# A transformer block's last projection ended in two column halves, and the last sum of each row's mean square moved to ScalarE

## The chip, the cores and the metric

One Trainium2 chip, one core. The time is device microseconds of one execution of the whole program, and smaller is better. The kernel before was run three times: 418.63, 420.02 and 420.79 us, median 420.02 us. One further execution was profiled.

## The reference

The program computes one transformer block on 256 tokens of width 1024, and a final normalisation. All arrays are float32. Cut to what matters here:

```
x  = x + gt_m * (gated attention branches @ w_out)          # 1024 x 1024
h2 = rms_norm(x, g_ffn) * (1 + sc_f) + sh_f
u  = causal_conv(h2 @ w_up)                                  # 1024 -> 5632
y  = (gelu(u_gate) * u_val) @ w_down                         # 2816 -> 1024
out = rms_norm(x + gt_f * y, g_final)
rms_norm(x, g) = x / sqrt(mean(x*x over the 1024 columns) + 1e-6) * g
```

## The kernel before

The 256 tokens are two tiles of 128 rows, t = 0 and t = 1, with the tokens on the partitions wherever a row is summed. Float32 operands are split into a high and a low part (`wh`, `wl` for weights, made on ScalarE and VectorE; `xh`, `xl` for activations), and a product is three matmuls: high times high, high times low, low times high (`mm3`, lines 181 to 185).

The weights come through a stream of units. One unit of the stages `out` and `down` is two blocks of 128 rows by 512 columns, so it takes 2 x 3 matmuls per token tile. `Stream.mm` runs one unit for one token tile; with a stage's last unit the stage's `finish` is started, which takes the sums out of PSUM. `Stream.ahead` issues loads and splits of later units before each step. A PSUM accumulator is one bank of 512 columns; four banks go round among the stages from `out` on.

`down` has two stages, `down0` for the output columns 0 to 511 and `down1` for 512 to 1023, with 11 units each. `down0` runs both token tiles unit by unit. `down1` runs through `staggered` with a lag of 4: tile 1 follows tile 0 by four units, so that tile 0's end falls beside the last four units (24 matmuls) of tile 1. The stage `out` and the first stage of `up` are staggered in the same way.

`residual` (line 939) takes columns out of PSUM: multiply by the gate row (line 940, VectorE), add to the residual `xr` (line 941, VectorE), square with a sum over the columns (line 942, ScalarE, a second small instruction reads the accumulator). `down_put` calls it for 512 columns in `down0` and twice for 256 columns in `down1`; each time a VectorE instruction of one column (line 1077) adds the scaled sum to the one before. Then GpSimd raises the mean to the power -0.5 (line 1085), ScalarE scales the columns 0 to 511, which already hold x times g (line 1086), VectorE makes the columns 512 to 1023 (line 1088), and SyncE and ScalarE issue one output DMA of 512 columns each (lines 1087 and 1090).

`rstd_of` (line 126) is the same end for the two earlier normalisations: VectorE adds two partial sums where there are two (line 130), scales and adds 1e-6 (line 131 or 133), GpSimd raises to the power (line 135). `square` and `turn` call it for the first normalisation at the program's start, `out_put` for the one between `out` and `up`. There the rows are scaled (line 959), transposed on TensorE (line 968), modulated (lines 976 and 979) and split (lines 153 and 154) for the first matmuls of `up`.

Up to the stage `out` each engine's order is the order of the text. From there on a planner sets it when the program is built: each engine takes, of the instructions that the planner's own clock holds ready, the one of highest priority, which is the earliest in the text unless a `high_priority` block lifts it. At run time each engine keeps that order.

Of the kernel before, what the change touches and what calls it, by code (L numbers as in the profile page):

```python
# [9 lines left out]
F32 = mybir.dt.float32  # L10
F32R = mybir.dt.float32r
AF = mybir.ActivationFunctionType
ALU = mybir.AluOpType
# [4 lines left out]
P = 128  # L18
D = 1024
# [34 lines left out]
def block_kernel(ctx: ExitStack, tc: tile.TileContext, x, c, w_ada, b_ada, g_mix, w_in, w_br_moba,  # L54
# [27 lines left out]
    def slot(tag, shape, dtype, name):  # L82
        return const.tile(shape, dtype, tag=tag, name=name)
# [11 lines left out]
    nc.vector.memset(ones, 1.0)  # L95
    neghalf = const.tile([P, 1], F32, name="neghalf")
    nc.vector.memset(neghalf, -0.5)
    ident = const.tile([P, P], F32, name="ident")
    nc.gpsimd.affine_select(ident, ones, pattern=[[1, P]], base=0, channel_multiplier=-1,
                            compare_op=ALU.is_equal, fill=0.0)  # L100
# [22 lines left out]
    warm_up(12)  # L123


    def rstd_of(ss, name):

        ms = small.tile([P, 1], F32, tag="ms", name=f"ms_{name}")
        if ss.shape[1] == 2:
            nc.vector.tensor_add(ms, ss[:, 0:1], ss[:, 1:2])  # L130
            nc.vector.tensor_scalar(ms, ms, 1.0 / D, EPS, op0=ALU.mult, op1=ALU.add)
        else:
            nc.vector.tensor_scalar(ms, ss, 1.0 / D, EPS, op0=ALU.mult, op1=ALU.add)
        r = small.tile([P, 1], F32, tag="rstd", name=f"rstd_{name}")
        nc.gpsimd.tensor_tensor(r, ms, neghalf, op=ALU.pow)
        return r
# [65 lines left out]
    class Stream:  # L202
# [67 lines left out]
        def mm(self, t, u):  # L270
# [15 lines left out]
            self.events += 1  # L286
            tick()

        def mm_fm(self, u, w):
            st, k0, _, _ = self.units[u]  # L290
            first, last = k0 == 0, k0 + 2 == st.kts
            prods = [(kk, sx, wi) for kk in range(2) for sx, wi in ((st.xh, w[0]), (st.xh, w[1]), (st.xl, w[0]))]
            if first:
                st.ps = [None, None]

            def product(n, f):
                kk, sx, wi = prods[n]
                nc.tensor.matmul(st.ps[f // 2][:, f % 2 * S:(f % 2 + 1) * S],  # L298
                                 wi[:, kk * 512 + f * P:kk * 512 + (f + 1) * P], sx(k0 + kk),
                                 start=first and n == 0 and f % 2 == 0, stop=last and n == 5 and f % 2 == 1)  # L300

            for half in range(2):
                if first:
                    st.ps[half] = self.bank(f"ps_{st.nm}_{half}")
                if first or last:
                    for n in range(6):
                        for f in (2 * half, 2 * half + 1):
                            product(n, f)
                else:
                    for n in range(3 * half, 3 * half + 3):  # L310
                        for f in range(4):
                            product(n, f)
                self.left[u] -= 1
# [53 lines left out]
            for t in (None,) if st_.fm or st_.half else range(NT):  # L367
                stream.mm(t, u)

    def staggered(us, lag):  # L370

        us = list(us)
        for i in range(len(us) + lag):
            if i >= lag:
                stream.mm(1, us[i - lag])
            if i < len(us):
                stream.mm(0, us[i])
# [9 lines left out]
    def square(t):  # L387
        sq = slot(f"xn{t}", [P, D], F32, f"sq{t}")
        ss = small.tile([P, 1], F32, tag="ss1", name=f"ss1_{t}")
        nc.scalar.activation(sq, xs[t], AF.Square, accum_out=ss)  # L390
        return ss

    def turn(t, ss):
# [540 lines left out]

    xr, xn = [None] * NT, [None] * NT
    ss2 = [small.tile([P, 2], F32, tag="ss2", name=f"ss2_{t}") for t in range(NT)]
    h2 = []

    def residual(t, ps, sl, row, ss, e):
        nc.vector.tensor_mul(e, ps, row[:, sl])  # L940
        nc.vector.tensor_add(xr[t][:, sl], xr[t][:, sl], e)
        nc.scalar.activation(e, xr[t][:, sl], AF.Square, accum_out=ss)

    def out_put(i):
        def put(t, ps):
            with tc.high_priority(offset=0):
# [2 lines left out]
                sl = slice(i * 512, (i + 1) * 512)  # L949
                residual(t, ps, sl, gt_m, ss2[t][:, i:i + 1], xn[t][:, sl])  # L950
            if i == 0:
                return
            if not h2:
                h2.extend(slot(n, [P, KT, S], F32R, f"{n}_") for n in ("h2h", "h2l"))
            with tc.high_priority(offset=200):
                r = rstd_of(ss2[t], f"n2_{t}")
                for half in range(2):
                    sl = slice(half * 512, (half + 1) * 512)
                    nc.vector.tensor_scalar(xn[t][:, sl], xr[t][:, sl], r, None, op0=ALU.mult)
# [103 lines left out]
                for g in range(NF // 2)]  # L1063

    def down_put(i):
        def put(t, ps):
            n = len(down_parts[i])
            for a, w in down_parts[i]:
                col = pre[t][1]
                e = small.tile([P, 512], F32, tag="hf", name=f"fy{t}{a}", bufs=3)[:, :w]  # L1070
                residual(t, ps[:, a - i * 512:a - i * 512 + w], slice(a, a + w), gt_f, ss3[t][:, col:col + 1], e)
                first = col == 0
                pre[t][1] += 1
                if first:
                    pre[t][2] = small.tile([P, 3], F32, tag="msx", name=f"ms3_{t}")
                ms = pre[t][2][:, col:col + 1]
                nc.vector.tensor_scalar(ms, ss3[t][:, col:col + 1], 1.0 / D, EPS if first else pre[t][0],
                                        op0=ALU.mult, op1=ALU.add)
                pre[t][0] = ms
            if i == 0:  # L1080
                yo[t] = slot(f"xn{t}", [P, D], F32, f"yo{t}")
                nc.vector.tensor_mul(yo[t][:, 0:512], xr[t][:, 0:512], gfin[:, 0:512])
                return
            rs = small.tile([P, 1], F32, tag="rstd", name=f"rstd_n3_{t}")
            nc.gpsimd.tensor_tensor(rs, pre[t][0], neghalf, op=ALU.pow)
            nc.scalar.mul(yo[t][:, 0:512], yo[t][:, 0:512], rs)
            nc.sync.dma_start(out[t * P:(t + 1) * P, 0:512], yo[t][:, 0:512])
            nc.vector.scalar_tensor_tensor(yo[t][:, 512:], xr[t][:, 512:], rs, gfin[:, 512:], op0=ALU.mult,
                                           op1=ALU.mult)
            nc.scalar.dma_start(out[t * P:(t + 1) * P, 512:], yo[t][:, 512:])  # L1090
            yield 1
        return put

    pre = [[None, 0, None] for _ in range(NT)]
    down_parts = [[(0, 512)], [(512, 256), (768, 256)]]
    yo = [None] * NT
    down_units = [stream.add(Stage(f"down{i}", NF, columns(w_down, i * 512), stacked(ah), stacked(al), down_put(i)))
                  for i in range(2)]
# [45 lines left out]
    nc.gpsimd.dma_start(gfin, bass.AP(tensor=g_final.tensor, offset=g_final.offset, ap=[[0, P], [1, D]]))  # L1144
    ss3.extend(small.tile([P, 3], F32, tag="ss3", name=f"ss3_{t}") for t in range(NT))
    together(down_units[0])
    staggered(down_units[1], 4)
    drain()


# [27 lines left out]
```

## Time and profile before

| | us |
|---|---|
| median of three runs | 420.02 |
| the three runs | 418.63 to 420.79 |
| the profiled execution's own time | 418.87 |
| its span, first to last instruction | 417.1 |
| mean granted TensorE clock, share of full speed | 0.995 |

The profile's times are those of the profiled execution, from the start of its span. In the rows, PE is TensorE's matmuls, DVE VectorE, ACT ScalarE, POOL GpSimd, and SPq and ACTq are the engines' own DMA issue. A row of the timeline gives start, length, engine, line, operation and shapes, a count where several follow one another, and in brackets how long the engine had been idle before and what ended that.

### The profile page before, as it was taken

To read this page: it belongs to the slowest core of one execution; us is meant where nothing else is said; L and a number is where in the kernel's file an instruction comes from. 1 tells how busy PE (TensorE), PEld (TensorE's weight loads), DVE (VectorE), ACT (ScalarE), POOL (GpSimd) and SP (SyncE) were. 2 spreads that over 40 slices of the span, in tenths; PEclk is the share of its full clock that TensorE was granted. 3 is DMA by queue.
4 is the path that set the end of the run, shared out by engine and by line. 5 is a ranking of instruction groups with operands and counts; after the bars stand their busy time and mean duration, and the time that the engine had idled before them with its cause. 6 is when DMAs were issued, how large, how long until landed. Compare 5 with 4: busy or idle time off the path is not lost.

```text
span 417.1 us, 7453 instructions
## 1 busy us (share of the span) xinstructions
PE 402.3 (96%) x2956; PEld 369.1 (88%) x2956; DVE 315.8 (76%) x474; ACT 253.9 (61%) x405; POOL 25.9 (6%) x64
## 2 busy tenths in 40 slices
PE   7999999999999999999979999999999999999992
PEld 6778899999999999999857999999999998888881
DVE  3645579788578979999597899999978888546433
ACT  4544477787697897816375658666766676343412
POOL 4500000000000110000330000000000000000000
PEclk9999999999999999999999999999999999999997
DMA  8999998977556875876957686877566555564002
GB/s 272 335 327 332 341 323 272 334 253 258 198 179 229 262 281 173 281 239 224 321 167 240 211 263 215 264 243 250 166 212 182 202 170 170 176 242 133 21 0 101
DMA packets 75082, 94.49 MB, mean 227 GB/s; under 512 B 2573, under 2 KB 61072, under 8 KB 75047
## 3 DMA queue, kind: packets, MB, share of 16 engines
q1 hardware_dynamic: 74135, 91.82, 68.2%
q10 hardware_dynamic: 576, 1.57, 1.0%
q0 software_dynamic: 336, 0.62, 0.4%
q8 instruction: 23, 0.38, 0.4%
q14 instruction: 12, 0.10, 0.1%
HBM read 92.94 MB, written 1.06 MB: 225 GB/s over the span
## 4 chain that ended last, share of the span: by engine, by line
PE 88%; SPq 3%; DMA 3%; DVE 3%; issue 1%; ACT 1%; POOL 0%; POOLq 0%; ACTq 0%
PE ps_up L298 27%; PE ps_down L185 15%; PE ps_ga L329 6%; PE ps_gb L329 6%; PE pA L472 4%; PE ps_out L185 4%; PE ps_vb L329 3%; PE ps_qb L329 3%; PE ps_yb L329 3%; PE ps_kb L329 3%; PE ps_ya L329 3%; DMA ada<-in_w_ada_dram 2%; PE ps_up L185 2%; PE pV L477 2%; SPq L449 2%; PE cs L457 1%
## 5 line engine op out<-in xcount | busy, mean ns | idle before, releaser
L143 ACT CAST wh_up<-raw_up 128x1024 fp32r<-128x1024 f32 x44 | 46.1, 1049 | 26.6 <-PE ps_up L298 21.5
L298 PE MATMUL ps_up<-h2h__2633,wh_up 128*128 128x256 f32 x320 | 57.7, 282 | 0.0
L298 PE MATMUL ps_up<-h2h__2633,wl_up 128*128 128x256 f32 x320 | 57.4, 281 | 0.0
L298 PE MATMUL ps_up<-h2l__2634,wh_up 128*128 128x256 f32 x320 | 57.4, 281 | 0.0
L148 DVE TENSOR_TENSOR wl_up<-raw_up,wh_up 128x1024 fp32r<-128x1024 f32 x42 | 50.9, 1220 | 7.0 <-ACT wh_up L143 6.9
L298 PEld LDWEIGHTS ps_up<-h2h__2633,wh_up 128*128 128x128 f32 x320 | 46.4, 188 | 0.2
L298 PEld LDWEIGHTS ps_up<-h2h__2633,wl_up 128*128 128x128 f32 x320 | 46.3, 188 | 0.0
L298 PEld LDWEIGHTS ps_up<-h2l__2634,wh_up 128*128 128x128 f32 x320 | 46.3, 188 | 0.0
L148 DVE TENSOR_TENSOR wl_down<-raw_down,wh_down 128x1024 fp32r<-128x1024 f32 x22 | 26.9, 1224 | 25.5 <-ACT wh_down L143 25.5
L143 ACT CAST wh_down<-raw_down 128x1024 fp32r<-128x1024 f32 x22 | 23.1, 1052 | 32.1 <-PE ps_down L185 23.6
L1040 DVE SCALAR_TENSOR_TENSOR cv<-ps_up,wc,cv 128x255 f32<-128x255 f32 (+1 forms) x80 | 34.6, 477 | 1.4 <-ACT cv L1034 0.8
L185 PE MATMUL ps_down<-wh_down,hl_a 128*128 128x512 f32 x88 | 34.8, 395 | 0.0
L185 PE MATMUL ps_down<-wl_down,hh_a 128*128 128x512 f32 x88 | 34.8, 395 | 0.0
L185 PE MATMUL ps_down<-wh_down,hh_a 128*128 128x512 f32 x88 | 34.8, 395 | 0.0
L1034 ACT ACTIVATE cv<-ps_up,vc,wc 128x256 f32<-128x256 f32 x40 | 20.4, 561 | 5.9 <-PE ps_up L298 5.9
L553 ACT CAST whA<-raw_wA 128x1024 fp32r<-128x1024 f32 (+1 forms) x9 | 8.6, 952 | 21.3 <-DMA raw_wA<-in_w_in_dram 21.3
L185 PEld LDWEIGHTS ps_down<-wh_down,hl_a 128*128 128x128 f32 x88 | 16.5, 188 | 4.0
L185 PEld LDWEIGHTS ps_down<-wh_down,hh_a 128*128 128x128 f32 x88 | 16.6, 188 | 3.9
L185 PEld LDWEIGHTS ps_down<-wl_down,hh_a 128*128 128x128 f32 x88 | 16.5, 188 | 3.9
L556 DVE TENSOR_TENSOR wlA<-raw_wA,whA 128x1024 fp32r<-128x1024 f32 x8 | 9.8, 1226 | 8.5 <-ACT whA L553 8.4
L329 PE MATMUL ps_gb<-hh,wh_gb 128*128 128x256 f32 x64 | 13.2, 288 | 0.0
L329 PE MATMUL ps_ga<-hh,wh_ga 128*128 128x256 f32 x64 | 13.2, 288 | 0.0
(280 smaller groups left out, 968.6 us busy)
## 6 DMA issues: line engine op xcount, KB each, us to landing
raw_up<-in_w_up_dram SPq DMA_DIRECT2D x44, 512.0 KB, 5.3
raw_down<-in_w_down_dram SPq DMA_DIRECT2D x10, 1024.0 KB, 4.9
ada<-in_w_ada_dram SPq DMA_DIRECT2D x16, 512.0 KB, 8.1
raw_wA<-in_w_in_dram SPq DMA_DIRECT2D x8, 768.0 KB, 9.4
raw_ga<-in_w_in_dram SPq DMA_DIRECT2D x4, 1024.0 KB, 9.8
ada_gtm<-in_w_ada_dram SPq DMA_DIRECT2D x8, 512.0 KB, 5.4
ada_shf<-in_w_ada_dram SPq DMA_DIRECT2D x8, 512.0 KB, 5.0
raw_gb<-in_w_in_dram SPq DMA_DIRECT2D x4, 1024.0 KB
```

Of the source, the lines that this page charges most:

```text
L143: nc.scalar.copy(wh, t[:, a:a + 1024])
L148: eng.tensor_sub(wl, t[:, a:a + 1024], wh.bitcast(F32))
L185: nc.tensor.matmul(ps, sx(k)[:, sl], w[:, c0:c0 + n], start=first and i == 0, stop=last and i == 2)
L298: nc.tensor.matmul(st.ps[f // 2][:, f % 2 * S:(f % 2 + 1) * S], wi[:, kk * 512 + f * P:kk * 512 + (f + 1) * P], sx(k0 + kk), start=first a ...
L329: nc.tensor.matmul(st.ps[:, f * S:(f + 1) * S], cols[:, a] if st.fm else x_[:, a], x_ if st.fm else cols, start=first and kk == n == f == ...
L449: nc.sync.dma_start(wws[j][:, :1536], w_in[j * P:(j + 1) * P, QA:QA + 1536])
L472: nc.tensor.matmul(psqk[f // 2][:, f % 2 * S:(f % 2 + 1) * S], wp[0][n == 2][:, f * P:(f + 1) * P], (hh, hl, hh)[n][:, j, :], start=j == 0 ...
L477: nc.tensor.matmul(psv[t], (hh, hl, hh)[n][:, j, t * P:(t + 1) * P], wp[1][n == 2][:, 0:512], start=j == 0 and n == 0, stop=j == KT - 1 an ...
L553: nc.scalar.copy(wh[i][:, a:a + n], wws[j][:, i * 1024 + a:i * 1024 + a + n])
L556: nc.vector.tensor_sub(wl[i][:, a:a + n], wws[j][:, i * 1024 + a:i * 1024 + a + n], wh[i][:, a:a + n].bitcast(F32))
L1034: nc.scalar.activation(ct[:, b, :], tp[:, b * S:(b + 1) * S], AF.Identity, bias=bconv[:, fb:fb + 1], scale=wc[:, 88 + fb:89 + fb])
L1040: nc.vector.scalar_tensor_tensor(ct[:, b, d:], tp[:, b * S:(b + 1) * S - d], wc[:, (2 - d) * 44 + fb:(2 - d) * 44 + fb + 1], ct[:, b, d:], ...
```

## The change

Token tile 1 of `down1` gets two PSUM banks of 256 columns each in place of one of 512. `staggered` gets a switch, `ends`, which only `down1` sets: while tile 0 still has units, tile 1 runs each unit as half 0 and then half 1, and its last four units run as half 0 of all four, then half 1 of all four. `finish` is run for half 0 as soon as half 0 has its last unit.

The squares are taken of x/32 (an immediate scale of the same ScalarE instruction), so that their sum is the mean already. The last step of the mean, a VectorE instruction before, is an Identity with a bias column on ScalarE: the bias is 1e-6, or the partial means before with 1e-6 added. That holds in all three normalisations. In the stage `out` one VectorE instruction per tile (`ms2`) adds 1e-6 to the first half's mean. In `down1`, x times g is made for the columns 512 to 1023 too, before the rows' factor is known, and the final scaling is split at column 448: ScalarE takes the columns 0 to 447, VectorE the other 576, and so do the two output DMAs.

```diff
+    def squares(o, x_, ss):
+        nc.scalar.activation(o, x_, AF.Square, scale=1.0 / math.isqrt(D), accum_out=ss)
+    def rstd_of(ss, name, more=None):
         ms = small.tile([P, 1], F32, tag="ms", name=f"ms_{name}")
-        if ss.shape[1] == 2:
-            nc.vector.tensor_add(ms, ss[:, 0:1], ss[:, 1:2])
-            nc.vector.tensor_scalar(ms, ms, 1.0 / D, EPS, op0=ALU.mult, op1=ALU.add)
-        else:
-            nc.vector.tensor_scalar(ms, ss, 1.0 / D, EPS, op0=ALU.mult, op1=ALU.add)
+        nc.scalar.activation(ms, ss, AF.Identity, bias=eps if more is None else more)
...
+        def mm_halves(self, us):
+            for half in range(2):
+                for u in us:
+                    while self.ahead(u):
+                        pass
+                    st, k0, _, _ = self.units[u]
+                    if k0 == 0:
+                        st.ps[1] = (st.ps[1] or []) + [self.bank(f"ps_{st.nm}_1{half}")]
+                    for kk in range(2):
+                        mm3(st.ps[1][half][:, 0:256], st.xh, st.xl, k0 + kk, 1, *self.w[u], kk * 512 + half * 256,
+                            k0 + kk == 0, k0 + kk == st.kts - 1)
+                    if k0 + 2 == st.kts:
+                        run(st.finish(1, [p_[:, 0:256] if i == half else None for i, p_ in enumerate(st.ps[1])]))
...
     def residual(t, ps, sl, row, ss, e):
         nc.vector.tensor_mul(e, ps, row[:, sl])
         nc.vector.tensor_add(xr[t][:, sl], xr[t][:, sl], e)
-        nc.scalar.activation(e, xr[t][:, sl], AF.Square, accum_out=ss)
+        squares(e, xr[t][:, sl], ss)
...
             if i == 0:
+                ms2[t] = small.tile([P, 1], F32, tag="ms2", name=f"ms2_{t}")
+                nc.vector.tensor_scalar(ms2[t], ss2[t][:, 0:1], EPS, None, op0=ALU.add)
                 return
...
-                r = rstd_of(ss2[t], f"n2_{t}")
+                r = rstd_of(ss2[t][:, 1:2], f"n2_{t}", ms2[t])
...
+        def part(t, ps, a, w):
+            col = a // 256 - (a > 0)
+            e = small.tile([P, 512], F32, tag="hf", name=f"fy{t}{a}", bufs=3)[:, :w]
+            sl = slice(a, a + w)
+            residual(t, ps, sl, gt_f, ss3[t][:, col:col + 1], e)
+            if a == 0:
+                yo[t] = slot(f"xn{t}", [P, D], F32, f"yo{t}")
+            nc.vector.tensor_mul(yo[t][:, sl], xr[t][:, sl], gfin[:, sl])
+            if col < 2:
+                ms = small.tile([P, 1], F32, tag=f"ms3{col}", name=f"ms3_{t}{col}")
+                nc.vector.tensor_scalar(ms, ss3[t][:, col:col + 1], pre[t] if col else EPS, None, op0=ALU.add)
+                pre[t] = ms
+                return
+            rs = rstd_of(ss3[t][:, col:col + 1], f"n3_{t}", pre[t])
+            nc.scalar.mul(yo[t][:, 0:CUT], yo[t][:, 0:CUT], rs)
+            nc.sync.dma_start(out[t * P:(t + 1) * P, 0:CUT], yo[t][:, 0:CUT])
+            nc.vector.tensor_scalar(yo[t][:, CUT:], yo[t][:, CUT:], rs, None, op0=ALU.mult)
+            nc.scalar.dma_start(out[t * P:(t + 1) * P, CUT:], yo[t][:, CUT:])
...
-    staggered(down_units[1], 4)
+    staggered(down_units[1], 4, ends=True)
```

## Rows read from the trace of the kernel before

**Rows 1.** The page: shares of the chain that ended last, by engine.

```profile
PE 88%; SPq 3%; DMA 3%; DVE 3%; issue 1%; ACT 1%; POOL 0%; POOLq 0%; ACTq 0%
```

**Rows 2.** The chain that ended last, from 395 us on: start, length, what.

```profile
394.94 14.71 PE ps_down L185 x63
...
409.67 0.76 DVE fy L940 x2
```

**Rows 3.** Timeline of the end: VectorE, ScalarE, GpSimd and the DMA issues.

```profile
404.07 0.76 DVE L940 TENSOR_TENSOR fy<-ps_down,gt_f 128x256 f32<-128x256 f32 x2 [4.64 <-PE ps_down L185]
...
407.87 0.36 ACTq L1090 DMA_DIRECT2D out_dram<-yo  x1
...
411.79 0.21 DVE L1077 TENSOR_SCALAR ms<-ss,ms 128x1 f32<-128x1 f32 x1 [0.18 <-ACT fy L942]
412.15 0.55 POOL L1085 TENSOR_TENSOR rstd_n<-ms,neghalf 128x1 f32<-128x1 f32 x1 [5.10 <-DVE ms L1077]
412.73 0.72 ACT L1086 ACTIVATE yo<-yo,rstd_n 128x512 f32<-128x512 f32 x1 [0.97 <-POOL rstd_n L1085]
...
413.52 0.35 ACTq L1090 DMA_DIRECT2D out_dram<-yo  x1
```

**Rows 4.** Groups by form: shapes, count, busy us, mean ns of one, idle before.

```profile
L508 ACT ACTIVATE ab<-h,vc 128x1 f32<-128x1 f32 x8 | 2.0, 251 | 0.0
L942 ACT ACTIVATE fy<-xr 128x256 f32<-128x256 f32 x4 | 1.6, 410 | 10.1 <-DVE xr L941 10.1
L1086 ACT ACTIVATE yo<-yo,rstd_n 128x512 f32<-128x512 f32 x2 | 1.4, 724 | 1.9 <-POOL rstd_n L1085 1.9
...
L959 DVE TENSOR_SCALAR xn<-xr,rstd_n 128x512 f32<-128x512 f32 x4 | 1.8, 484 | 1.1 <-POOL rstd_n L135 1.1
L940 DVE TENSOR_TENSOR fy<-ps_down,gt_f 128x256 f32<-128x256 f32 x4 | 1.5, 420 | 6.5 <-PE ps_down L185 6.5
```

**Rows 5.** Timeline of TensorE in the up stage, matmuls of 256 columns.

```profile
318.11 0.64 PE L298 MATMUL ps_up<-h2h__2633,wh_up 128*128 128x256 f32 x4
...
322.37 0.39 PE L298 MATMUL ps_up<-h2h__2633,wh_up 128*128 128x256 f32 x2
```

**Rows 6.** The chain that ended last, in the stage of the second gates.

```profile
144.71 4.46 PE ps_gb L329 x36
```

**Rows 7.** DMA issues: queue, count, KB each, median us to landing.

```profile
raw_down<-in_w_down_dram SPq DMA_DIRECT2D x2, 512.0 KB, 3.7
...
out_dram<-yo ACTq DMA_DIRECT2D x2, 256.0 KB, 2.7
```

**Rows 8.** Timeline between out and up: VectorE.

```profile
208.12 0.69 DVE L940 TENSOR_TENSOR xn<-ps_out,gt_m 128x512 f32<-128x512 f32 x1 [3.20 <-PE ps_out L185]
208.85 0.69 DVE L941 TENSOR_TENSOR xr<-xr,xn 128x512 f32<-128x512 f32 x1
...
219.74 0.16 DVE L130 TENSOR_TENSOR ms_n<-ss 128x1 f32<-128x1 f32 x1
219.82 1.23 DVE L148 TENSOR_TENSOR wl_up<-raw_up,wh_up 128x1024 fp32r<-128x1024 f32 x1
220.96 0.15 DVE L131 TENSOR_SCALAR ms_n<-ms_n 128x1 f32<-128x1 f32 x1
```

**Rows 9.** The same stretch: ScalarE and GpSimd.

```profile
212.95 0.18 ACT L942 ACTIVATION_READ_ACCUMULATOR xn<-xr 128x1 f32 x1
213.04 1.98 ACT L143 CAST wh_up<-raw_up 128x1024 fp32r<-128x1024 f32 x2
...
213.85 0.57 POOL L135 TENSOR_TENSOR rstd_n<-ms_n,neghalf 128x1 f32<-128x1 f32 x1 [2.02 <-DVE ms_n L131]
```

**Rows 10.** The same stretch: TensorE.

```profile
214.99 1.16 PE L968 MATMUL h2t<-ident,xn 128*128 128x128 f32 x8 [0.62 <-DVE xn L959]
...
219.13 0.50 PE L185 MATMUL ps_up<-wh_up,h2h__2633 128*128 128x512 f32 x1 [2.28 <-ACT h2h__2633 L153]
```

**Rows 11.** The chain that ended last, in the program's first 30 us.

```profile
17.59 9.49 DMA ada<-in_w_ada_dram
```

More of the change, by code (lines that the diff above doesn't have):

```diff
@@ L97, in block_kernel @@
     nc.vector.memset(neghalf, -0.5)
+    eps = const.tile([P, 1], F32, name="eps")
+    nc.vector.memset(eps, EPS)
+    assert math.isqrt(D) ** 2 == D
     ident = const.tile([P, P], F32, name="ident")
@@ L123, in block_kernel @@
     warm_up(12)
-    def rstd_of(ss, name):
+    def squares(o, x_, ss):
+        nc.scalar.activation(o, x_, AF.Square, scale=1.0 / math.isqrt(D), accum_out=ss)
+    def rstd_of(ss, name, more=None):
         ms = small.tile([P, 1], F32, tag="ms", name=f"ms_{name}")
-        if ss.shape[1] == 2:
-            nc.vector.tensor_add(ms, ss[:, 0:1], ss[:, 1:2])
-            nc.vector.tensor_scalar(ms, ms, 1.0 / D, EPS, op0=ALU.mult, op1=ALU.add)
-        else:
-            nc.vector.tensor_scalar(ms, ss, 1.0 / D, EPS, op0=ALU.mult, op1=ALU.add)
+        nc.scalar.activation(ms, ss, AF.Identity, bias=eps if more is None else more)
         r = small.tile([P, 1], F32, tag="rstd", name=f"rstd_{name}")
@@ L287, in mm @@
             tick()
+        def mm_halves(self, us):
[11 more added lines that the diff above has]
+                        run(st.finish(1, [p_[:, 0:256] if i == half else None for i, p_ in enumerate(st.ps[1])]))
+                    if half:
+                        self.left[u] -= 1
+                        self.events += 1
+                        tick()
         def mm_fm(self, u, w):
@@ L368, in together, with staggered @@
                 stream.mm(t, u)
-    def staggered(us, lag):
+    def staggered(us, lag, ends=False):
         us = list(us)
         for i in range(len(us) + lag):
-            if i >= lag:
+            if ends and i >= lag:
+                if i < len(us):
+                    stream.mm_halves(us[i - lag:i - lag + 1])
+                elif i == len(us):
+                    stream.mm_halves(us[i - lag:])
+            elif i >= lag:
                 stream.mm(1, us[i - lag])
@@ L389, in square @@
         ss = small.tile([P, 1], F32, tag="ss1", name=f"ss1_{t}")
-        nc.scalar.activation(sq, xs[t], AF.Square, accum_out=ss)
+        squares(sq, xs[t], ss)
         return ss
@@ L936, in block_kernel @@
     ss2 = [small.tile([P, 2], F32, tag="ss2", name=f"ss2_{t}") for t in range(NT)]
-    h2 = []
+    h2, ms2 = [], [None] * NT
     def residual(t, ps, sl, row, ss, e):
@@ L1065, in down_put @@
     def down_put(i):
-        def put(t, ps):
[L1067 to L1079, printed above, removed]
-            if i == 0:
[L1081 to L1090, printed above, removed]
@@ L1091, in put @@
+        def put(t, ps):
+            if i == 0:
+                part(t, ps, 0, 512)
+            else:
+                for b, p_ in enumerate(ps if t else (ps[:, 0:256], ps[:, 256:512])):
+                    if p_ is not None:
+                        part(t, p_, 512 + b * 256, 256)
             yield 1
         return put
-    pre = [[None, 0, None] for _ in range(NT)]
-    down_parts = [[(0, 512)], [(512, 256), (768, 256)]]
+    CUT = 448
+    pre = [None] * NT
     yo = [None] * NT
```

## The prediction

> **What bounds the kernel now.** I read the page's chain first, then the chain's last 20 us, the timeline of that end, the groups by form for prices, and last the stretch between `out` and `up`. TensorE holds 88% of the chain that ended last [rows 1]. So only three things count: what TensorE itself does per matmul, where it stands idle, and what follows its last matmul. The last matmul lets go at 394.94 + 14.71 = 409.65 us; VectorE starts on its sums at 409.67 [rows 2]. The last output DMA is issued at 413.52 [rows 3]. These 3.87 us are the tail, and nothing covers them. After the issue the transfer takes some 2.7 us to land [rows 7].
>
> The second open place lies between `out` and `up`: TensorE waits 0.62 us for the scaled rows of tile 0 before it transposes them, and 2.28 us for their split before `up` starts [rows 10]. A microsecond gained or lost in that chain is one of the kernel. The first normalisation, which the change touches too, is no such place: at 17.59 the chain still waits 9.49 us for a load of `w_ada` [rows 11], long after the rows were scaled. I cost that edit, the 1e-6 column at the start and the scale 1/32 (an immediate of the same instruction) at nothing; if the loads gave no cover, the first would cost 0.1 us per tile, 0.25 us for the Identity against 0.15 to 0.21 for the VectorE step [rows 3, 4, 8].
>
> **The tail, after TensorE's end.** Only 256 columns are left then. Step by step, from 409.65 as zero:
> - multiply: starts at 0.02, 0.42 long [rows 2, 4], ends 0.44.
> - add: a dependent VectorE instruction follows 0.04 later (208.12 + 0.69 to 208.85 [rows 8]); as long as the multiply, it ends at 0.90.
> - square and reading of its sum: 0.04 + 0.41 + 0.18 [rows 4, 9], ends 1.53.
> - the mean on ScalarE: the trace has no such Identity in this place. The nearest row is another instruction of one column with a bias column, 0.25 us [rows 4]; the VectorE step that it replaces took 0.21 [rows 3]. I take 0.25, after a hand-over of 0.03: ends 1.81. Bounds: 0.15 (the shortest one-column step of rows 8) and 0.41 (a square of 256 columns, rows 4).
> - the power: 0.15 from the VectorE step's end (412.00) to GpSimd's start at 412.15, and 0.55 itself [rows 3]: ends 2.51.
> - the scaling: 0.03 later. ScalarE's 448 columns lie between 0.41 (256 columns, no scale column) and 0.724 (512 with one) [rows 4], much nearer the second; per column (0.724 - 0.410)/256 = 1.2 ns, so 0.65. VectorE's 576 columns are a plain scaling now: 0.484 for 512 [rows 4], about 0.54, hidden beside it. Ends 3.19.
> - the DMA issue, 0.05 after that: 3.24.
>
> The tail falls from 3.87 to 3.24, by 0.63 us. Two halves of multiply, add and square that ran in turn are now one. With the bounds of the Identity (-0.10, +0.16) and of the scaling (-0.24, +0.07) the gain is 0.40 to 0.97.
>
> A sentence apart: the Trainium skill (ScalarE: Activation LUTs, section What ACT_TABLE_LOAD costs) gives an ACTIVATE with a bias column 280 ns plus 0.83 ns per column. The row has 251 ns; by the page the tail would gain 0.03 us less.
>
> The last DMA grows from 256 to 288 KB and its neighbour shrinks to 224. A load of 512 KB took 3.7 us to land against 2.7 for the 256 KB store [rows 7], 1.0 per 256 KB, so 32 KB are 0.12 us for one queue alone. Both queues end together, with the bytes unchanged; I take +0.06, between -0.12 and +0.12.
>
> **The cover of half 0.** Tile 0's matmuls end near 404.05 (VectorE starts at 404.07) and its last issue is at 407.87 [rows 3]. Half 0 of tile 1 ends 24 x 0.118 = 2.8 us after tile 0, at 406.9, half 1 at 409.7. Half 0 needs VectorE for multiply, add, x times g (3 x 0.42) and a small step that waits for ScalarE, with 0.41 + 0.18 of squaring between [rows 4, 9]: about 2.1 us. If VectorE first ends tile 0's scaling, near 407.6, half 0 is through at about 409.3 to 409.7. So it just fits. If it doesn't, the small step stands in VectorE's queue ahead of the last multiply, which waits for it; that would cost 0.1 to 0.4 us. Tile 0's own extra (two products with g, 2 x 0.42) lies in VectorE's wait for the power.
>
> **TensorE's matmuls.** Tile 1 of `down1` has 11 units x 6 = 66 matmuls of 512 columns; now 132 of 256, each with its own weight load. In `down1` 63 matmuls took 14.71 us [rows 2], 0.2335 each. In `up`, where each matmul of 256 columns has its own load as well, 36 took 322.37 - 318.11 = 4.26 us [rows 5], 0.1183 each. A pair costs 0.2366, 0.0031 more, 66 pairs 0.20 us. Bounds: 0 (the columns are the same) and, by the second gates' stretch, 4.46/36 = 0.124 [rows 6] with its change-overs in it, 66 x (0.248 - 0.2335) = 0.95 us. I take 0.20. The bank for half 1 is the one that tile 0 of `down0` gave back; the VectorE reads that free it ended over 5 us of staggering earlier, so no wait.
>
> A rule weighed here, and needed by nothing else: the Trainium skill (TensorE: Matmul & The Clock Gate, section Back-to-back issue gap) puts streams of weight load and matmul at about 81 ns for 128 columns and 131 ns for 512, so that halving the columns would not halve the time. By a straight line, an estimate, 256 columns would be 98 ns and the 66 pairs 4.3 us dearer. This trace disagrees: 118 and 233.5 ns, which is by columns.
>
> **Between `out` and `up`.** VectorE loses two small steps per tile in the chain (0.15 each) and gets one (`ms2`) beside it; ScalarE gets one of 0.25. What counts is where the planner puts the Identity. The rows speak both ways. For tile 1 it had put a split of 1.23 us between the two dependent VectorE steps (219.74, 219.82, 220.96 [rows 8]), and that is gone. For tile 0, ScalarE has two casts, 1.98 us, right behind the reading of the sum [rows 9]; if the planner again holds a dependent step back and fills in, a cast comes before the Identity. But a late tile 0 lets the last matmuls of `out`, and with them tile 1, come forward into TensorE's 0.62 us of idle time. I take 0, between -0.3 and +0.6 for this term; the ends are worked out below.
>
> **Sum.** -0.63 + 0.06 + 0.20 + 0 = -0.37 us. The profiled execution took 418.87 us, which makes 418.5. It is 1.15 below the median of the three runs; against that median the forecast is 420.02 - 0.37 = 419.65, so **419.6 us**. The runs spread over 2.2 us, and a measurement of this kernel can't tell less than 0.5%, 2.1 us, from no change.
>
> **Rivals.**
> 1. *The Identity comes straight behind the reading.* Reading ends 213.13 [rows 9], Identity 213.41, the power starts 213.56 instead of 213.85: 0.29 earlier, and TensorE's idle time shrinks by it. With the sum: -0.66, 419.4. If the replanned order also takes a cast (0.99, half of the pair in rows 9) out of the chain behind the transposes, where TensorE waits 2.28: -1.65, 418.4. For it: the block there has high priority. Against: the filler of rows 8.
> 2. *The Identity stands behind casts* (the slower side). Behind one (to 214.03) the power starts at 214.46, 0.61 later; behind both (to 215.02) at 215.45, 1.60 later. TensorE waits in this chain already [rows 10], so it passes on. The kernel is slower as soon as it is over 0.37: 420.3 with one, 421.25 with two. For it: rows 8. Against: priority, and what comes forward instead.
> 3. *The halves don't end apart*, because the planner's order lets half 0's work pile up behind tile 0's tail, or mixes the halves. The tail then stays 3.87 but for 0.07 of the shorter scaling; with +0.06 and +0.20: 420.2. For it: the cover above has hardly any slack. Against: VectorE's work between the two ends is (6 x 0.42 + 0.21 + 0.54) for tile 0 and 3 x 0.42 + 0.21 for half 0, 4.7 of 5.7 us.
> 4. *256 columns cost by the matmul, not by the column.* If 132 matmuls went at the long pace of rows 6 and missed more at each bank change, up to +0.95: 420.4. The 36 in a row of rows 5 speak against it.
>
> **Chances.** Forecast 0.40, rival 1 0.26, rival 2 0.20, rival 3 0.10, rival 4 0.04. The range: rival 1's far end 418.4 and rival 2's far end 421.25, widened below by 0.6 for the spread of the runs; above, half of rival 2 lies far inside: **417.8 to 421.2**. The forecast's own range, with tail -0.97 to -0.40, DMA +-0.12, TensorE 0 to 0.95 and the border's -0.3 to +0.6, taken together rather than all at one end, is 418.8 to 420.6. Faster by over 0.5% (below 417.9) needs rival 1's far end and a run from the lower part of the spread: 0.12. Slower by over 0.5% (above 422.1) needs two casts and an unlucky spread: 0.06. No change: 0.82.
>
> **What would show it.** In the changed kernel's trace: 24 matmuls of 256 columns between the end of half 0 and of half 1, 2.8 us; from the last matmul to the last issue 3.24 us with one multiply, add and square; one-column Identities of 0.25 us on ScalarE; the power starting 0.15 us after the last; tile 1's pairs at 0.2366 us. Between `out` and `up`, the start of the power (213.85 now) and TensorE's two waits decide between rivals 1 and 2. I am wrong if the tail doesn't shrink by at least 0.4 us, if VectorE's multiply of half 1 starts over 0.1 us after the last matmul, or if the border moves by more than 0.6 us.

## The result: 2.0 us slower, and the profile after

The changed kernel's median is 421.64 us (421.04 to 422.08, 9 runs); the kernel before, beside it on the same chip, 419.63 us (418.63 to 420.79, 9 runs). The ratio of the executions is 1.0053, 95% interval 1.0041 to 1.0065 (the quotient of the two medians is 1.0048). The forecast was 419.6 us and the range ended at 421.2: the prediction was wrong, on the side of its rival 2. The profiled execution of the changed kernel took 421.82 us, span 420.1, mean granted clock 0.990 (before: 418.87, 417.1, 0.995).

Two traces are compared best by the same six marks on TensorE and the DMA queues: the first matmul of `out`, the first of `up`, the first of `up` with 256 columns, the first of `down`, the end of the last matmul, the end of the last DMA issue. In `up` the first 48 matmuls have 512 columns; "first of 256" ends that part. Marks and differences in us:

| | first of `out` | `out` to `up` | `up` to its first of 256 | from there to `down` | `down` | tail, to the end of the last issue |
|---|---|---|---|---|---|---|
| before | 192.60 | 26.53 | 13.30 | 115.50 | 61.71 | 4.23 |
| after | 192.44 | 28.37 | 15.67 | 115.51 | 61.44 | 3.55 |
| difference | -0.16 | **+1.84** | **+2.37** | +0.01 | -0.27 | **-0.68** |

With -0.11 from the last issue to the end of the span (3.23 and 3.12) the row sums to 3.00, the difference of the spans. The medians are only 2.01 apart: the profiled execution of before was 0.76 under its median here, that of after 0.18 above.

So the tail did what was forecast, and all of the loss in these two traces lies at the border between `out` and `up`. First the tail, in the timeline of the changed kernel (start, length, engine, line, operation; in brackets the idle time before and its end):

```profile
413.15 0.28 PE L188 MATMUL ps_down<-wh_down,hl_a 128*128 128x256 f32 x1
...
412.77 0.21 DVE L1106 TENSOR_SCALAR ms<-ss,ms 128x1 f32<-128x1 f32 x1
413.46 0.42 DVE L968 TENSOR_TENSOR fy<-ps_down,gt_f 128x256 f32<-128x256 f32 x1 [0.47 <-PE ps_down L188]
413.92 0.43 DVE L969 TENSOR_TENSOR xr<-xr,fy 128x256 f32<-128x256 f32 x1
...
414.38 0.42 ACT L131 ACTIVATE fy<-xr 128x256 f32<-128x256 f32 x1 [1.64 <-DVE xr L969]
414.70 0.19 ACT L131 ACTIVATION_READ_ACCUMULATOR fy<-xr 128x1 f32 x1
414.92 0.29 ACT L136 ACTIVATE ms_n<-ss,ms 128x1 f32<-128x1 f32 x1
...
415.35 0.55 POOL L138 TENSOR_TENSOR rstd_n<-ms_n,neghalf 128x1 f32<-128x1 f32 x1 [4.50 <-issue]
...
415.93 0.67 ACT L1110 ACTIVATE yo<-yo,rstd_n 128x448 f32<-128x448 f32 x1 [0.71 <-POOL rstd_n L138]
416.48 0.35 ACTq L1113 DMA_DIRECT2D out_dram<-yo  x1
...
411.58 5.40 SPq L1111 DMA_DIRECT2D out_dram<-yo  x2
```

Against [rows 2, 3]: one multiply, add and square after the last matmul, not two. Half 0's last step ends at 412.98, 0.45 us before TensorE's end (413.15 + 0.28), and the multiply starts 0.03 after it: the cover held. The last row is both of SyncE's issues; the second ends at 416.98.

Now the border. The next two fences are the changed kernel's timeline of tile 0's chain and of TensorE:

```profile
212.80 0.18 ACT L131 ACTIVATION_READ_ACCUMULATOR xn<-xr 128x1 f32 x1
212.89 1.03 ACT L146 CAST wh_up<-raw_up 128x1024 fp32r<-128x1024 f32 x1
213.83 0.29 ACT L136 ACTIVATE ms_n<-ss,ms 128x1 f32<-128x1 f32 x1
...
213.96 1.23 DVE L151 TENSOR_TENSOR wl_up<-raw_up,wh_up 128x1024 fp32r<-128x1024 f32 x1 [0.54 <-ACT wh_up L146]
215.65 0.88 DVE L989 TENSOR_SCALAR xn<-xr,rstd_n 128x512 f32<-128x512 f32 x2 [0.47 <-POOL rstd_n L138]
216.44 0.68 DVE L968 TENSOR_TENSOR xn<-ps_out,gt_m 128x512 f32<-128x512 f32 x1
217.04 1.21 DVE L151 TENSOR_TENSOR wl_up<-raw_up,wh_up 128x1024 fp32r<-128x1024 f32 x1
218.18 0.72 DVE L1006 TENSOR_SCALAR h2f<-h2t,ab 128x128 f32<-128x128 f32 x2
...
214.19 1.42 POOL L138 TENSOR_TENSOR rstd_n<-ms_n,neghalf 128x1 f32<-128x1 f32 x1 [2.52 <-ACT ms_n L136]
```

```profile
214.51 0.39 PE L188 MATMUL ps_out<-wh_out,zl 128*128 128x512 f32 x1
216.19 1.09 PE L998 MATMUL h2t<-ident,xn 128*128 128x128 f32 x8 [1.29 <-DVE xn L989]
220.81 0.80 PE L188 MATMUL ps_up<-wh_up,h2h__2639 128*128 128x512 f32 x1 [3.53 <-ACT h2h__2639 L156]
```

The reading of tile 0's sum ends at 212.98, as long after `out`'s first matmul as before (20.54 and 20.53 us). From there to `up`'s first matmul it takes 7.83 us; before it took 6.00 [rows 9, 10]. Three steps make the 1.83:
- the planner put one cast of 1.03 us between the reading and the Identity. The power starts 1.21 us after the reading, not 0.72: +0.49;
- the power takes 1.42 us, not 0.57 [rows 9]: it runs beside VectorE's weight split, which that cast released: +0.85;
- on VectorE a multiply and a split (0.68 and 1.21 us) now stand between the scaled rows and the first modulation; before, it was the split alone. The first modulation starts 1.99 us after the transposes, not 1.39, and `up` 4.62 us after them, not 4.14 [rows 10]: +0.48.

The kernel before's timeline of VectorE in the same place, its two steps of the mean first:

```profile
213.43 0.15 DVE L130 TENSOR_TENSOR ms_n<-ss 128x1 f32<-128x1 f32 x1
213.62 0.15 DVE L131 TENSOR_SCALAR ms_n<-ms_n 128x1 f32<-128x1 f32 x1
...
215.25 1.22 DVE L148 TENSOR_TENSOR wl_up<-raw_up,wh_up 128x1024 fp32r<-128x1024 f32 x1
216.38 0.74 DVE L976 TENSOR_SCALAR h2f<-h2t,ab 128x128 f32<-128x128 f32 x2
```

TensorE waits 1.29 and 3.53 us, not 0.62 and 2.28. After that its clock is lower. The stretches of 5 us (TensorE's busy time is the second number, its granted clock the third from the end, full speed 1.00), first before, then after:

```profile
210.00:215.00 5.00, 4.38 (x20) 3.21 (x18) 4.25 (x7) 3.94 (x7) 2.39 (x2) 1.00 0.32 104
215.00:220.00 5.00, 2.72 (x14) 1.72 (x15) 4.91 (x11) 4.00 (x10) 0.62 (x1) 1.00 0.72 228
220.00:225.00 5.00, 4.74 (x24) 3.72 (x25) 4.36 (x8) 1.57 (x5) 0.94 (x1) 1.00 0.51 192
```

```profile
210.00:215.00 5.00, 4.90 (x22) 3.63 (x20) 4.43 (x5) 3.94 (x9) 2.48 (x2) 1.00 0.38 115
215.00:220.00 5.00, 1.09 (x8) 0.86 (x8) 4.54 (x10) 3.17 (x7) 1.23 (x2) 1.00 1.00 338
220.00:225.00 5.00, 3.94 (x13) 2.92 (x14) 3.98 (x8) 2.55 (x8) 0.66 (x1) 0.52 0.65 209
225.00:230.00 5.00, 5.00 (x19) 3.98 (x18) 3.59 (x6) 1.83 (x4) 0.00 (x0) 0.80 0.47 178
230.00:235.00 5.00, 5.00 (x23) 3.99 (x23) 1.57 (x2) 2.77 (x4) 0.00 (x0) 1.00 0.01 2
```

TensorE was busy 1.09 of the 5 us before 220; in the next 5 us it was granted 0.52, about the lower of its two levels (1.2 of 2.4 GHz). From 225 to 230 it was granted 0.80, and 1.00 from then on. The +2.37 lies in these 10 us.

### The profile page after: what moved, and what is told of

Its sections match the earlier page's. It is cut to its first block, busy times and chain, and to the rows that moved or that the text cites. A ratio compares the mean times of both kernels' runs of the same rounds, so it can differ in the third digit from the quotient of the medians.

```text
span 420.1 us, 7587 instructions
## 1 busy us (share of the span) xinstructions
PE 405.2 (96%) x3022; PEld 375.5 (89%) x3022; DVE 316.6 (75%) x473; ACT 255.7 (61%) x411; POOL 26.6 (6%) x64
## 4 chain that ended last, share of the span: by engine, by line
PE 92%; DVE 2%; issue 2%; DMA 1%; ACT 1%; POOL 1%; POOLq 0%; ACTq 0%
PE ps_up L320 27%; PE ps_down L188 14%; PE pA L500 6%; PE ps_ga L351 6%; PE ps_gb L351 6%; PE ps_out L188 4%; PE ps_up L188 3%; PE ps_vb L351 3%; PE ps_qb L351 3%; PE ps_yb L351 3%; PE ps_ya L351 3%; PE pV L505 3%; PE ps_kb L351 3%; PE cs L485 2%; DMA x<-in_x_dram 1%
## 5 line engine op out<-in xcount | busy, mean ns | idle before, releaser
L188 PE MATMUL ps_down<-wh_down,hh_a 128*128 128x512 f32 (+1 forms) x110 | 38.3, 348 | 0.0
L188 PE MATMUL ps_down<-wh_down,hl_a 128*128 128x512 f32 (+1 forms) x110 | 38.3, 348 | 0.0
L188 PE MATMUL ps_down<-wl_down,hh_a 128*128 128x512 f32 (+1 forms) x110 | 38.2, 347 | 0.0
L188 PEld LDWEIGHTS ps_down<-wh_down,hl_a 128*128 128x128 f32 x110 | 20.7, 188 | 2.9
L188 PEld LDWEIGHTS ps_down<-wl_down,hh_a 128*128 128x128 f32 x110 | 20.7, 188 | 2.8
L188 PEld LDWEIGHTS ps_down<-wh_down,hh_a 128*128 128x128 f32 x110 | 20.7, 188 | 2.7
L138 POOL TENSOR_TENSOR rstd_n<-ms_n,neghalf 128x1 f32<-128x1 f32 x6 | 4.3, 719 | 203.8 <-ACT ms_n L136 199.3
```

## The experiments

Medians in us, each against the kernel before on the same chip; the ratio's 95% interval in brackets. The columns on the right come from the profiled execution of each, by the marks above. e11 and e12, single executions, follow in the text.

| | median | ratio | `out` to `up` | `up` to 256 | tail |
|---|---|---|---|---|---|
| after | 421.64 | 1.0053 [1.0041, 1.0065] | 28.37 | 15.67 | 3.55 |
| e1 down stage's part alone | 418.48 | 0.9970 [0.9956, 0.9984] | 26.54 | 14.38 | 3.56 |
| e2 sums' part alone | 422.56 | 1.0062 [1.0048, 1.0076] | 28.37 | 15.34 | 4.23 |
| e3 last sum on VectorE | 418.35 | 0.9961 [0.9945, 0.9976] | 26.47 | 14.34 | 3.56 |
| e9 e3 only between `out` and `up` | 418.55 | 0.9977 [0.9964, 0.9990] | 26.47 | 14.12 | 3.54 |
| e10 e3 only at the start | 421.47 | 1.0048 [1.0029, 1.0068] | 28.38 | 14.38 | 3.55 |
| e4 after, TensorE kept busy | 420.05 | 1.0011 [0.9999, 1.0022] | 28.37 | 13.57 | 3.55 |
| e5 Identity ahead of the casts | 419.47 | 1.0012 [0.9996, 1.0028] | 29.05 | 14.38 | 3.56 |
| e8 e1 without the halves | 418.59 | 0.9987 [0.9973, 1.0001] | 26.54 | 14.07 | 4.17 |
| e6 before, TensorE kept busy | 419.61 | 0.9999 [0.9984, 1.0014] | 26.54 | 13.29 | 4.24 |
| e7 e3, TensorE kept busy | 417.62 | 0.9959 [0.9944, 0.9974] | 26.48 | 13.24 | 3.55 |

### Which part: e1, e2, e9, e10

**e1**, the down stage's edits alone:

```diff
-        nc.scalar.activation(ms, ss, AF.Identity, bias=eps if more is None else more)
+        if more is not None:
+            nc.scalar.activation(ms, ss, AF.Identity, bias=more)
+        elif ss.shape[1] == 2:
+            nc.vector.tensor_add(ms, ss[:, 0:1], ss[:, 1:2])
+            nc.vector.tensor_scalar(ms, ms, 1.0, EPS, op0=ALU.mult, op1=ALU.add)
+        else:
+            nc.vector.tensor_scalar(ms, ss, 1.0, EPS, op0=ALU.mult, op1=ALU.add)
...
```

> The changed kernel with the mean of the first two normalisations on VectorE again, as before (one add, one scale-and-add); down1's halves, its Identity and the split at column 448 stay. Theory (the loss lies between out and up, where the planner's order and then the TensorE clock changed; the tail's gain is real): up's first matmul 2.6 to 2.8 us after out's last, clock 1.00 there, tail 3.2 us, time 0.7 us under the kernel before, 418.9. Rival (the halves cost in down, by twice as many matmuls and weight loads): at or over the kernel before, 419.6 to 421.6.

418.48, a gain of 1.3 us on before's 419.74 there. The clock is a miss: it fell to 0.66 in e1's trace (220 to 225 us), at a border as long as before's. **e2**, the mirror: the down stage as before, the Identity in the first two normalisations.

> The changed kernel with the stage down1 of before (one bank of 512 columns, mean on VectorE, cut at 512); the first two normalisations keep their Identity on ScalarE. Theory: the whole loss without the tail's gain: up's first matmul 6.2 us after out's last, clock 0.5 for some 6 us after it, tail 3.87, time 2.0 + 0.7 = 2.7 us over the kernel before, 422.3. Rival (halves): within 0.5 us of the kernel before, 419.1 to 420.1.

422.56, a loss of 2.8 on the same 419.74. The loss goes with the sums, the gain with the down stage; together they make 1.6, and the whole change 2.0. **e9** and **e10** divide the sums between the two places (e9's edit is shown; e10 is the other way round):

```diff
-        nc.scalar.activation(ms, ss, AF.Identity, bias=eps if more is None else more)
+        if name[:2] == "n2":
+            nc.vector.tensor_scalar(ms, ss, more, None, op0=ALU.add)
+        else:
+            nc.scalar.activation(ms, ss, AF.Identity, bias=eps if more is None else more)
```

> The changed kernel with the normalisation between out and up ending its mean in a VectorE step again; the first normalisation and the last one keep the ScalarE Identity. Theory (the whole loss comes from the Identity between out and up; the first one is covered by the load of w_ada): like the kernel with the VectorE step in both, 418.0 to 418.8 us, scaled rows of tile 0 transposed near 215.0, up started near 219.1. Rival (the first normalisation's later start, 0.93 us in the traces, is part of the loss): 419.2 to 419.8 us, with every stage from the first transposes on later by about 0.9 us.

> The changed kernel with the first normalisation ending its mean in a VectorE step again; the one between out and up and the last one keep the ScalarE Identity. Theory (the Identity between out and up alone makes the loss): 421.2 to 422.1 us, as the changed kernel, with up's first matmul 6 us or more after out's last and TensorE's clock at the lower level after it. Rival (the first normalisation makes part of it): 420.3 to 420.9 us.

418.55 and 421.47 (e10's traced run, 420.36, is its shortest, with the clock at 0.66 for 5 us only): one Identity, the one between `out` and `up`, makes the loss. The Identity of the first normalisation shows no cost, as the prediction had it: the first matmul behind it came at 14.53 us in after and 13.60 in before, but at 14.82 in e3 with VectorE there, and `out` began no later in after than in before (192.44, 192.60). The chain of e9, in its timeline, with a VectorE step in the Identity's place:

```profile
212.82 0.19 ACT L131 ACTIVATION_READ_ACCUMULATOR xn<-xr 128x1 f32 x1
212.91 1.98 ACT L149 CAST wh_up<-raw_up 128x1024 fp32r<-128x1024 f32 x2
213.37 0.20 DVE L137 TENSOR_SCALAR ms_n<-ss,ms 128x1 f32<-128x1 f32 x1
213.65 0.57 POOL L141 TENSOR_TENSOR rstd_n<-ms_n,neghalf 128x1 f32<-128x1 f32 x1 [1.95 <-DVE ms_n L137]
...
218.94 0.67 PE L191 MATMUL ps_up<-wh_up,h2h__2639 128*128 128x512 f32 x1 [2.12 <-ACT h2h__2639 L159]
```

The casts stand right behind the reading here too, but now no step of the chain is behind them, and the power runs alone.

### The place or the instruction: e3, e5

**e3** puts the VectorE step in both earlier normalisations, and leaves the rest of the change:

```diff
+        if name[:2] == "n3":
+            nc.scalar.activation(ms, ss, AF.Identity, bias=more)
+        else:
+            nc.vector.tensor_scalar(ms, ss, EPS if more is None else more, None, op0=ALU.add)
```

> The changed kernel with only the engine of the last step changed in the first two normalisations: VectorE adds the half mean that ms2 prepared, one step where the kernel before had two. Theory (what cost was the Identity's place in ScalarE's queue, behind a cast): the power of tile 0 starts within 0.3 us of the kernel before, up starts 2.3 to 2.9 us after out's last matmul, clock 1.00, time 0.7 to 1.0 us under the kernel before, 418.6 to 418.9. Rival (any replanning of that stretch costs, since the old order was tuned): 420 to 422.

418.35, 3.3 us under after. Its clock, too, is a miss: 0.68 from 220 to 225 us. **e5** keeps the Identity and orders the two casts behind it:

```diff
...
-        nc.scalar.copy(wh, t[:, a:a + 1024])
+        with tc.issue_after(behind[0]) if behind else ExitStack():
+            nc.scalar.copy(wh, t[:, a:a + 1024])
...
```

> The changed kernel, where the two weight casts that the planner had put around tile 0's Identity between out and up are ordered behind it (an issue-order edge, no wait). Theory (not the Identity as such cost, but its place behind a cast and what the planner then put ahead of the chain): the Identity starts within 0.1 us of the reading's end, the power starts 0.3 to 1.0 us earlier than in the changed kernel and takes 0.57 us, up starts at most 2.9 us after out's last matmul; time at or under the kernel that only has the tail, 417.8 to 418.9. Rival (a ScalarE step in that chain costs wherever it stands): 420 or more.

419.47, between the theory and the rival. In e5's trace (of its longest run, 421.90 us) the Identity stands where rival 1 of the prediction had it, and the power is short:

```profile
213.49 0.19 ACT L131 ACTIVATION_READ_ACCUMULATOR xn<-xr 128x1 f32 x1
213.71 0.30 ACT L138 ACTIVATE ms_n<-ss,ms 128x1 f32<-128x1 f32 x1
...
214.08 0.57 POOL L142 TENSOR_TENSOR rstd_n<-ms_n,neghalf 128x1 f32<-128x1 f32 x1 [1.71 <-ACT ms_n L138]
...
215.23 1.09 PE L1007 MATMUL h2t<-ident,xn 128*128 128x128 f32 x8 [1.93 <-DVE xn L998]
...
222.20 0.50 PE L197 MATMUL ps_up<-wh_up,h2h__2639 128*128 128x512 f32 x1 [2.00 <-ACT h2h__2639 L165]
```

From the reading's end to the power it takes 0.40 us (after: 1.21). But the whole order is planned anew: the transposes now stand ahead of the last ten matmuls of `out`, TensorE waits 1.93 us for them and runs those ten at a granted 0.66 (215 to 220 us). So e5 shows that the first two of the three steps go away with the casts, but not that the Identity itself would be free: the three of e5's runs with a mean clock of 0.997 took 418.56 to 419.14 us, two of e3's with 0.996 and 0.997 took 417.66 and 417.43 (on another chip).

### The clock's share: e4

Matmuls whose sums nothing reads, behind tile 0's transposes:

```diff
+            if t == 0:
+                with tc.high_priority(offset=400):
+                    warm2 = bank(sm, "warm2")
+                    for i_ in range(26):
+                        nc.tensor.matmul(warm2[:, 0:S], onesr, zh[:, i_ % KT, :], start=True, stop=True)
```

> The changed kernel with 26 matmuls of 256 columns, 3.06 us, whose sums nobody reads, right behind tile 0's transposes between out and up, where TensorE waited 3.53 us. Theory (about 2.4 of the 4.1 us lost there are the halved clock, and the clock fell because TensorE stood idle): the granted clock stays 1.00 in that stretch, up's 48 matmuls of 512 columns take 13.3 us again and not 15.7, time 2.4 us under the changed kernel, 419.2. Rival (the wait alone counts, the clock costs nothing or falls all the same): 421.6 as the changed kernel, or more if the 26 matmuls delay up's first.

```profile
215.00:220.00 5.00, 3.71 (x29) 3.25 (x28) 4.54 (x8) 3.30 (x6) 2.04 (x2) 1.00 0.96 304
220.00:225.00 5.00, 3.85 (x26) 3.06 (x25) 4.53 (x10) 3.13 (x8) 0.65 (x1) 1.00 0.74 239
225.00:230.00 5.00, 5.00 (x23) 4.04 (x22) 3.12 (x7) 2.37 (x5) 0.00 (x0) 1.00 0.64 238
```

The clock stays at 1.00, and `up` to its first of 256 takes 13.57 us, 2.10 less than in after; `out` to `up` keeps its 28.37. The medians moved by 1.6 (by the ratios 1.8), not the 2.4 expected: e4's executions may come later to `out`, as the traced one did (193.32 us), and after's other executions were up to 0.8 shorter than its traced one. So in the traces the loss of 4.21 at the border is 2.10 of clock and 2.11 of waiting: 1.84, and the 0.27 that e4's 13.57 is over before's 13.30, where tile 1's transposes wait 0.72 us, not 0.26.

### The halves: e8

e1 with tile 1 of `down1` in one bank again:

```diff
-                for b, p_ in enumerate(ps if t else (ps[:, 0:256], ps[:, 256:512])):
+                for b, p_ in enumerate((ps[:, 0:256], ps[:, 256:512])):
...
-    staggered(down_units[1], 4, ends=True)
+    staggered(down_units[1], 4)
```

> The kernel that only has the tail (mean of the first two normalisations on VectorE), but with down1's tile 1 in one bank of 512 columns, ended at once; Identity, early product with g and the split at column 448 stay. Theory (the halves carry the tail's gain): from TensorE's end to the last issue 3.75 to 3.9 us, as in the kernel before, time 0.5 to 0.7 us over the kernel with the halves, 419.1. Rival (the Identity or the early product with g carry it): 3.2 to 3.4 us and 418.5.

```profile
408.99 0.40 PE L194 MATMUL ps_down<-wh_down,hl_a 128*128 128x512 f32 x1
...
409.43 0.76 DVE L974 TENSOR_TENSOR fy<-ps_down,gt_f 128x256 f32<-128x256 f32 x2 [2.02 <-PE ps_down L194]
410.10 0.75 DVE L975 TENSOR_TENSOR xr<-xr,fy 128x256 f32<-128x256 f32 x2
```

Two multiplies and two adds again behind TensorE's end, and a tail of 4.17 against 3.56 in e1: the halves carry 0.61 of the tail's 0.68. The ratios (0.9987 and 0.9970, on two chips) are 0.7 us apart, but their intervals overlap.

The halves also cost something in `down`: 61.76 us without them, 62.00 with them in e1. Both traces take 30.8 us for `down0`; from `down1`'s first matmul to VectorE's last multiply it is 31.01 without halves and 31.24 with them. Two matmuls of 256 columns take 2 x 0.1185 us there, one of 512 takes 0.2333; over 66 pairs that is 0.24. In the seven other kernels with halves `down` took only 61.43 or 61.44 (61.70 to 61.77 in the five others without), but this isn't the halves' doing: the gain lies in `down0`, which has the same matmuls in every kernel. It took 30.42 or 30.43 us in these seven, since in its second half they follow each other in 0.229 us, not 0.2333. What speeds them isn't shown.

### Does the kernel before lose clock there too: e6, e7, e11, e12

The runs of before differ in mean granted clock: beside e5 to e8 it was 0.994 or more in 12 (median 418.73 us) and less in 18 (419.78). Both traced executions of it are of the first kind. If the others lose clock after the 2.28 us of [rows 10], filling that wait should help. **e6** puts 16 unread matmuls there, **e7** the same into e3:

```diff
+            if i == 1 and t == 1:
+                warm2 = bank(sm, "warm2")
+                for i_ in range(16):
+                    nc.tensor.matmul(warm2[:, 0:S], onesr, zh[:, i_ % KT, :], start=True, stop=True)
```

> The kernel before with 16 matmuls of 256 columns, 1.9 us, whose sums nobody reads, between out's last matmul and up's first, where TensorE waited 2.28 us. Theory (the kernel before loses clock at the same place in most executions, though not in the one profiled; its runs lie in two groups, mean clock 0.991 to 0.993 and 0.994 to 0.995, about 419.9 and 418.6 us): clock 0.995 or more in all runs, median 418.6. Rival (the groups have another cause, the idle time there never costs clock in the kernel before): 419.7, or later by what the fill delays.

> The kernel with VectorE's one step between out and up, the halves at the end, and the same 16 matmuls as fill. Theory: both gains add: the tail's 0.65 us and the clock kept; 417.4 to 417.7, as its two runs without a clock loss (417.43 and 417.66). Rival (the fill delays up as much as the clock gives): 418.3 as without it.

e6 is a miss: the clock is 1.00 in its trace up to TensorE's end, and 0.993 to 0.997 on average in its runs, and yet 419.61, no gain. Its trace came to `out` at 193.46, 0.86 later than before's, with a wait in the attention part that before's trace doesn't have:

```profile
162.90 0.50 PE L636 MATMUL po_s<-al,vbh 128*128 128x512 f32 x1 [0.94 <-DVE al L744]
```

e7 is the best kernel of all, 417.62, but not to be told from e3 by the ratio. It and e4 both keep the clock, and only e4 has the Identity in that chain (their added matmuls, 16 and 26, differ in number and place): their ratios are 2.2 us apart, as are their traces from `out` to the first of 256 (39.72 and 41.94). So the waiting that the Identity brings shows in the medians too. **e11** and **e12** are one more traced execution each of before and of e6:

> The kernel before once more, for a second trace of it. Theory (most of its executions lose part of the clock after the wait of 2.28 us ahead of up, the traced one did not): a granted clock below 1.00 in the 10 us after up's start and about 14.0 to 14.4 us from up's first matmul to its first of 256 columns, against 13.30 in the trace before; from out's first matmul to up's first 26.5 us as there. Rival (it keeps its clock, and the spread comes from elsewhere): 13.2 to 13.4 us, and out's first matmul at another time than 192.60 by as much as the execution is longer.

> The kernel before with the 16 unread matmuls between out and up once more, for a second trace. Theory (the late start of out, 193.46 us in its first trace, was that execution's own): out's first matmul between 191.5 and 192.8, and the time between 418.0 and 419.0. Rival (the added matmuls move the program's start or the attention branches later in each execution): out's first matmul at 193.2 us or later and about 419.5. Both: 13.2 to 13.4 us from up's first matmul to its first of 256 columns, 26.5 us from out's first to up's first.

e11 took 418.34 us: `out` at 192.09, 26.52 to `up`, 13.30 from there, clock 1.00 up to TensorE's end. Its theory missed, since this execution too kept its clock; so the loss in before's other runs isn't shown. It is likely: e1 and e8 keep before's order and waits at this border (26.54 us), their mean clocks, 0.993 and 0.991, are those of before's longer runs, and in their traces the clock fell there. TensorE's stretches, e1 first, then e8:

```profile
220.00:225.00 5.00, 5.00 (x20) 0.66 0.40 137
```

```profile
215.00:220.00 5.00, 2.72 (x9) 0.79 0.71 235
220.00:225.00 5.00, 5.00 (x25) 0.86 0.36 125
```

If so, the traces of before and after, where only the second lost clock, overstate what the change costs in clock between the medians.

e12 took 419.22: `out` at 192.95, 13.29 in `up`, and again a wait at 162 us, of 0.32. That lies between theory and rival. The wait doesn't go with the added matmuls: e5, without any, has it (0.29), as has e4 (0.77), and e7, with them, hasn't. The four traces that have it came last to `out`, 192.95 to 193.46 us; all others came between 191.50 and 192.66. What brings it stays open.

## Why the prediction was wrong

The step that failed is the border: "I take 0, between -0.3 and +0.6 for this term". It was +4.21 in the traces. The worst price in the prediction, rival 2's, stopped at the power's start and held the rest of the chain fixed; what followed from the cast on the other engines, and TensorE's clock, were put at nothing without a reason. Point by point:

- **What bounds the kernel.** Right: the border was named as the second open place, where "a microsecond gained or lost in that chain is one of the kernel". It was more than one: in the traces the waiting cost 2.11, and the clock 2.10 on top.
- **Rival 2, with one cast.** Its mechanism came: the planner filled the ScalarE with a cast between the two dependent steps, as [rows 8] had warned. From the reading's end the power started 0.49 later; the prediction said 0.61. The rows shown in the prediction spoke for it, and the priority was only argued; but in the same trace the planner had put nothing between tile 0's own two steps (213.43, 213.62), so that 0.20 was too low can't be said from that trace. The price stopped at the power's start. Missing were the power's length beside the split, +0.85, VectorE's new order, +0.48, and the clock. The prediction added the cast's delay to a chain that it held otherwise fixed.
- **What comes forward.** "The last matmuls of `out` ... come forward into TensorE's 0.62 us of idle time" did happen (`out`'s last matmul started at 214.51, not 216.46), and it gained nothing: those matmuls were cover for the second wait, and 0.70 of the 1.25 us by which it grew is that cover gone.
- **The clock.** No term stood for it. The trace of before shows 1.00 here, after a wait of 2.28 us, and the prediction took that as given for any order. With 0.62 and 2.28 us of waiting 1.00 was kept in that trace; with 1.29 and 3.53 it was not. Nor was it in e1 and e8 with the same waits as before: one trace at 1.00 was no ground to take it as given even for the old order.
- **The tail.** Right: 3.24 forecast, 3.19 measured to the last issue (416.62, SyncE's second: 411.58 + 5.40 less its own 0.36). The Identity took 0.29 (0.25 taken), the power 0.55, ScalarE's 448 columns 0.67 (0.65). A part of the closeness is luck: from the add's end to the end of the square's reading it took 0.54, not 0.63, since the two overlap, and the other steps together 0.04 more than forecast. The cover of half 0 held, with 0.45 us to spare.
- **The DMA.** +0.06 forecast; from the last issue's end to the span's end -0.11.
- **TensorE's pairs.** +0.20 forecast; `down` was 0.27 shorter. The price was right: the last eight matmuls of 256 columns start within 0.83 us (412.32 to 413.15), 0.118 each, and between e8 and e1 the halves cost 0.23. The stage is shorter by `down0`, 30.43 us and not 30.80, whose matmuls the change doesn't touch; no row of the prediction could show that.
- **The first normalisation.** Costed at nothing: no cost shows (e9, e10).
- **The two medians.** The forecast stood on 420.02; beside the changed kernel, before's median was 419.63. Of the miss of 2.0 us this explains nothing, it would have made it larger by 0.4.

Without the one Identity (e9) the ratio is 0.9977, and 0.9977 x 419.66 = 418.70, 0.96 under before (0.4 to 1.5 by the interval): the tail, with the rest of the change, is a gain.

## What to carry to other kernels

Where a planner orders an engine, a step moved onto that engine has the price of whatever is put in front of it, and of the order that follows from it on the other engines; look for what the planner does now between two dependent steps of one engine, and price that case to the end of the chain, not to the first delayed step. Price a longer wait of TensorE at more than its length: ask what the clock does after it, and don't take full speed for granted from one trace of a like wait: here it was kept in two traces and lost in four. Split a change into its places early: one run per place (e1, e9, e10) settled here what no reading of the whole could.

## What the runs showed of the hardware

- GpSimd's power of one column takes 0.55 to 0.57 us alone, and 1.42 in after beside VectorE's split of 1024 columns (213.96 to 215.19): it ended 0.42 after the split. In e9 tile 1's power beside a split took 1.47, and ended 0.44 after it. The other way round, VectorE's add of 512 columns took 2.13 us in after (210.10 to 212.23) beside GpSimd's own split (209.16 to 211.68), and 0.69 alone. The Trainium skill (SBUF — State Buffer, section Who interferes with whom) says that a VectorE instruction with two inputs in SBUF and a GpSimd instruction that reads SBUF exclude each other, and that the later one waits for the end of the earlier. These rows agree: what the later one took after the earlier had ended, 0.42 and 0.55 us, is most of its length alone (0.57 and 0.69).
- TensorE's clock after a wait isn't the same in each execution: after 2.1 to 2.3 us of waiting it stayed at 1.00 in before's two traces, and fell to 0.86 in e8, 0.75 in e9, 0.68 in e3 and 0.66 in e1 (220 to 225 us). After 3.5 us it fell to 0.66 in e10, 0.52 in after and 0.50 in e2. With the wait filled it stayed at 1.00 there, in the four traces of e4, e6, e7 and e12.
- The same matmuls of 512 columns, in the second half of `down0`, followed each other in 0.2333 us in seven kernels (before and e1 among them) and in 0.229 in seven others (after among them), at a granted clock of 1.00 in e1 as in after. What sets the pace isn't shown.
